# Weight sums by accumulating transfers, ready x parts, one-instruction SiLU and gate rows ahead, in a one-core hybrid decoder layer

## The chip, the core and the metric

The kernel runs on one core of a Trainium2 chip. Its engines run side by side, each through its own list of instructions: TensorE (PE, matrix products), VectorE (DVE), ScalarE (ACT), GpSimd (POOL, here mostly an issuer of transfers) and SyncE (SP, which only issues transfers). An instruction waits for the semaphores of what it depends on, and everything behind it on its engine waits too. The metric is the device time of one execution, in microseconds; the shorter the better.

## The reference: what is computed

One layer for 1024 tokens of width 1024, in float32. The input is normalised and modulated by a conditioning vector to h. One projection of h gives ten pieces: q, f, i and z of an HGRN2 mixer (eight heads), q, k, v, z and a low-rank decay of a gated linear attention (GLA, four heads), and two merge gates.

```python
mod = c_act @ ada_w[l] + ada_b[l]
shift, scale, gate = jnp.split(mod, 3, axis=-1)
h = rms_norm(x, norm_w[l]) * (1.0 + scale[:, None, :]) + shift[:, None, :]
proj = h @ w_in[l]
hq, hf, hi, hz, gq, gk, gv, gz, ga, mg = jnp.split(proj, IN_OFFSETS, axis=-1)
y_h = hgrn2_branch(hq, hf, hi, hz, lb_all[l], hgrn_norm_w[l])
y_g = gla_branch(gq, gk, gv, gz, ga, gla_alpha_w[l], gla_alpha_b[l], gla_norm_w[l])
u_h = y_h @ w_branch[l, 0]
u_g = y_g @ w_branch[l, 1]
mg = jax.nn.sigmoid(mg.reshape(B, T, N_BRANCH, D_MODEL))
merged = mg[:, :, 0] * u_h + mg[:, :, 1] * u_g
x = x + gate[:, None, :] * (merged @ w_out[l])
```

Both mixers are causal linear attentions with a decay per channel (`S = diag(a) S + k v^T`, `o = S^T q`), normalised and multiplied by `silu(z)`; HGRN's q is `silu(hq)`, its k is `(1 - lb) sigmoid(-hf)`. The last step is an RMS norm of x.

## The kernel before

**Products.** Every float32 factor is split in two parts, hi (an ACT cast) and lo (a DVE subtraction, `split` and `pinned_split`, L211 and L212), and a product is hi·hi + hi·lo + lo·hi, so three matmuls. The large products (v and i, the merge gates, the two branches, w_out) are also cut in 2 x 2 blocks and computed with seven block products instead of eight, in the order `PRODUCTS` = 1, 2, 5, 3, 6, 7, 4. Products 1, 2 and 3 use a plain block of h; 5, 7, 6 and 4 use a difference of blocks of h ("x sum", in DRAM as `fx`), and 5, 7, 6 and 3 use a sum of weight blocks.

**Stages on PE, in order.** The head (modulation, transposes of x, h); the q and k features of GLA (L396); V stage 0 (L1899: v of GLA, from 111 us); GLA's z features and the first attentions (L607, scores L665 and L698, outputs L832, L834); V stage 1 (L1899: i of HGRN, about 308 to 405); then the q, f and z features of eight HGRN heads with their attentions (to 778); then the last stages, groups (b, p) of 48 matmuls (L1351) over four column blocks b, the first at 779 us; w_out (L1528); the end norm.

**What sets the order.** `Stream.go` runs a list of jobs (features and V jobs) on PE. `Stream.ahead` issues the loads (SP) and the splits (ACT, DVE) of coming jobs, some jobs ahead and only if enough of the SBUF slots (`S`, 46 of 4 KB per partition) are free. `Stream.weave` advances two tracks by small steps after each unit of PE work: the side track (attention of the current head) and the back track (weight sums, gate row). Each step of a track is a piece of DVE, ACT or transfer work that is thereby put between the others in program order; `held` (`keep_in_program_order`) pins it there. A scheduler orders the rest by priority. Each `yield n` of the back track says after how many units the next step comes.

**The parts that the change touches.**
- `new_factors` (L1161) names the DRAM tiles `fx`. `Vjob.prep` makes the x sums in V stage 0 by a DVE subtraction (`make_factor`, L1739) and stores each by POOL (L1740). V stage 1 and column block 0 of the last stages load them again as float32 (L1843, `fetch_factor`) and split them (L211/L212, L1270/L1271).
- `v_sums` and `prepare` with `weight_sums` load weight blocks by SP, add them on DVE (L1754 to L1760, L1195 to L1201) and store the sums by POOL (L1762, L1203).
- `silu_done` (L967, L968) takes a sigmoid on ACT and multiplies on DVE. The k of HGRN is scaled on DVE (L1104).
- `gate_side` (L1066 to L1083) computes the gate row: eight rows of 512 KB are loaded one at a time, each taken into a DVE multiply-add (L1072), then four matmuls (L1083).
- In V stage 0 PE's results in PSUM are taken out by `Vstage.after` (L1782 to L1810); for product 7 by a DVE addition (L1810), and only then may product 4 start in the same bank.

SP's and POOL's transfers use eight semaphores each in turn, so a transfer waits for the landing of the one eight before it on its queue.

Of the kernel before, what the change touches and what calls it, by code (L numbers as in the profile page):

```python
# [89 lines left out]
def hybrid_trunk_kernel(  # L90
# [117 lines left out]
    def pinned_split(src, hi=None, lo=None):  # L208
        if hi is None:
            hi, lo = (S.get(list(src.shape[1:]), F32R) for _ in range(2))  # L210
        held(nc.scalar.copy(hi, src))  # L211
        nc.vector.tensor_sub(lo, src, hi.bitcast(F32))  # L212
        return hi, lo
# [399 lines left out]
    class Feat:  # L613

        raws, parts, more = 1, 2, 0
# [225 lines left out]
    class Stream:  # L841
# [26 lines left out]
        def go(self, loads=2, preps=1):  # L868
            n = len(self.jobs)
            for i, job in enumerate(self.jobs):  # L870
                self.ahead(i, loads + 2 * job.more, 0)
                for u, _ in enumerate(job.run()):
                    if job.calls(u):
                        self.ahead(i, loads + 2 * job.more, preps + (job.more if u else 0))
# [87 lines left out]
    def silu_done(store, key):  # L962
        def f(ps):
            s = S.get([T])
            for th in range(2):
                sl = slice(th * 512, th * 512 + 512)
                nc.scalar.activation(s[:, sl], ps[th], AF.Sigmoid)  # L967
                nc.vector.tensor_mul(s[:, sl], s[:, sl], ps[th])  # L968
# [93 lines left out]
    def gate_side():  # L1062
# [3 lines left out]
        for k in range(KT):  # L1066
            b = S.get([D])
            nc.sync.dma_start(b, ada_w[0, k * P:(k + 1) * P, 2 * D:3 * D])
            if k == 0:
                nc.vector.tensor_scalar_mul(gacc, b, cs[:, 0:1])  # L1070
            else:
                nc.vector.scalar_tensor_tensor(gacc, b, cs[:, k:k + 1], gacc, ALU.mult, ALU.add)  # L1072
            S.free(b)
            yield 1
# [20 lines left out]
    def hf_done(h):  # L1095
        def fn(ps):
# [7 lines left out]
            nc.vector.tensor_scalar_mul(k, k, oml[:, h:h + 1])  # L1104
# [56 lines left out]
    def new_factors(acts, name):  # L1161
        f = {}
        for p, kh, half in ((1, 0, 0), (2, 1, 0), (3, 1, 1)):
            f[p] = [part_of(acts, kh, half, kk) for kk in range(2)]
        for p in (1, 2, 3, 5, 6, 7, 4):
            if p not in f:
                f[p] = [dp.tile([P, T], F32, name=f"{name}{p}{kk}") for kk in range(2)]
        return f

    f_x = new_factors(h_d, "fx")  # L1170
# [7 lines left out]
    w_sums = [[[dp.tile([P, T], F32, name=f"ws{b}{j}{i}") for i in range(4)] for j in range(2)] for b in range(4)]  # L1178
# [3 lines left out]

    def load_blocks(b, i):
        src = sources[b][i]
        x = [S.get([4, 2, P]) for _ in range(2)]
        for kh in range(2):
            nc.sync.dma_start(x[kh].rearrange("p k a f -> p k (a f)"),
                              src[kh * 512:(kh + 1) * 512, :].rearrange("(k p) f -> p k f", p=P))
        return x

    def weight_sums(b, i, x1, x2):
        s1, s2 = S.get([2, 4, P]), S.get([2, 4, P])
        parts = {5: s1[:, 0], 6: s1[:, 1], 3: s2[:, 0], 7: s2[:, 1]}
        add = nc.vector.tensor_add
        held(add(parts[7], x1[:, :, 0], x1[:, :, 1]))  # L1195
        yield 1
        held(add(parts[5], x1[:, :, 1], x2[:, :, 1]))
        yield 1
        held(add(parts[6], parts[7], x2[:, :, 1]))
        yield 1  # L1200
        held(add(parts[3], parts[6], x2[:, :, 0]))  # L1201
        for p, q in SUMS.items():
            nc.gpsimd.dma_start(w_sums[b][i // 2][q][:, i % 2 * 512:i % 2 * 512 + 512],  # L1203
                                parts[p].rearrange("p k f -> p (k f)"))
        S.free(x1, x2)
        S.free(s1, s2, sent=True)
        summed_up.add((b, i))

    def prepare():
        todo = [(b, i) for b in range(4) for i in range(4)]  # L1210
        blocks_of = {}
        for n in range(len(todo) + 1):
            while n < len(todo) and (len(S.free_list) < 11 or paused[0]):
                yield 1
            if n < len(todo):
                blocks_of[n] = load_blocks(*todo[n])
            if n:
                yield from weight_sums(*todo[n - 1], *blocks_of.pop(n - 1))
            yield 7
# [3 lines left out]
    raw_f, raw_w, wt = {}, {}, {}  # L1223
    GROUPS = [(b, p) for b in range(4) for p in PRODUCTS]
    BUILT = [g for g in GROUPS if g[0] != 1]
# [6 lines left out]

    def fetch_factor(g):
        b, p = g
        raw_f[g] = [S.get([T]) for _ in range(2)]
        for kk in range(2):
            nc.sync.dma_start(raw_f[g][kk], f_x[p][kk])
# [39 lines left out]
    def load_duo(b, p, j):  # L1277

        t = raw_w[b, p, j] = S.get([2, 512])
        if p in SUMS:  # L1280
            assert {(b, 2 * j), (b, 2 * j + 1)} <= summed_up
            nc.sync.dma_start(t.rearrange("p a f -> p (a f)"), w_sums[b][j][SUMS[p]])
# [175 lines left out]
    for g in BUILT[1:]:  # L1458
        n = GROUPS.index(g)
        after(*GROUPS[n - 1], 0, lambda g=g: build(g))  # L1460
        if n > 1 and g[0] == 0:
            after(*GROUPS[n - 2], 2, lambda g=g: fetch_factor(g))
# [254 lines left out]
    vs_d = {p: [dp.tile([P, T], F32, name=f"vs{p}{kk}") for kk in range(2)] for p in SUMS}  # L1717
    summed_v = set()
    W_AT = {1: (0, 0), 2: (1, 0), 5: (0, 1), 3: (1, 0), 6: (0, 1), 7: (0, 0), 4: (1, 1)}
    RAW_X = {1: (0, 0), 2: (1, 0), 3: (1, 1)}  # L1720
# [16 lines left out]
    def make_factor(p, kk):  # L1737
        dst, x, y = {5: ("11", "12", "11"), 7: ("12", "12", "22"), 6: ("22", "22", "11"), 4: ("21", "21", "22")}[p]
        held(nc.vector.tensor_sub(xq[dst][kk], xq[x][kk], xq[y][kk]))  # L1739
        nc.gpsimd.dma_start(f_x[p][kk], xq[dst][kk].rearrange("p a t -> p (a t)"))  # L1740

    def v_sums():

        add = nc.vector.tensor_add
        for kk in range(2):
            while len(S.free_list) < 9:
# [248 lines left out]
```

## Time and profile before

| what | value |
|---|---|
| median of 3 runs | 1176.65 us (1176.1 to 1178.35) |
| the profiled execution, its own time | 1178.0 us |
| its span in the trace | 1176.2 us |
| matmul clock granted | 0.996 |
| POOL transfers of weight sums (L1203) | 64, 545 ns each to issue |
| DMA, 16 engines, mean rate | 188 GB/s, 221.44 MB |

The profile shows one execution. Busy time says how much an engine did, not whether anyone waited for it. PE is the engine that is always needed, so the useful views are those that say when PE stood still and who released it. An engine's timeline row has the start, the duration, the operation and, in brackets, how long the engine was idle before and which engine's work ended that.

### The profile page before, as it was taken

Reading aid. Unit: us, or ns where it says so; the run is one execution under the profiler, and the core shown is the slowest. Engines: PE = TensorE matmul, PEld = TensorE weight load, DVE = VectorE, ACT = ScalarE, POOL = GpSimd, SP = SyncE. Lnnn points to the kernel's source line nnn. Section 1 sums busy time; section 2 is a strip of 40 time slices with the busy share of each in tenths; the row PEclk is TensorE's granted clock in tenths of the full one; section 3 lists DMA queues with packets and bytes.
Section 4 is the critical chain, followed back from the end, with each engine's and each line's share of the span. In section 5 each row is a group of like instructions: output and inputs, shape, how many; then the busy total and the mean of one; then the engine's idle time right before and its main releaser. Section 6 shows DMA issues by size and latency. Waiting matters only on the chain.

```text
span 1176.2 us, 20432 instructions
## 1 busy us (share of the span) xinstructions
PE 1156.2 (98%) x8137; PEld 953.1 (81%) x8137; DVE 849.6 (72%) x1347; ACT 589.5 (50%) x903; POOL 125.0 (11%) x261
## 2 busy tenths in 40 slices
PE   7999999999999999999999999999999999999997
PEld 5777888888888788888888878888888888888886
DVE  4754778567665946897897798795643866988994
ACT  4675464663465535433433425567543644534654
POOL 4121111000100212111111010001110000000000
PEclk8999999999999999999999999999999999999999
DMA  9846445255675856565555453247699846434523
GB/s 319 279 149 233 161 170 189 77 165 171 207 260 177 279 189 201 171 203 173 174 184 188 134 205 112 91 162 241 196 314 298 274 156 215 130 108 162 187 90 134
DMA packets 150802, 221.44 MB, mean 188 GB/s; under 512 B 9052, under 2 KB 107410, under 8 KB 150707
## 3 DMA queue, kind: packets, MB, share of 16 engines
q1 hardware_dynamic: 132114, 158.37, 43.2%
q0 software_dynamic: 18544, 61.76, 13.6%
q8 instruction: 64, 1.05, 0.4%
q14 instruction: 32, 0.25, 0.1%
q10 hardware_dynamic: 48, 0.01, 0.0%
HBM read 154.57 MB, written 65.54 MB: 187 GB/s over the span
## 4 chain that ended last, share of the span: by engine, by line
PE 64%; issue 25%; DVE 4%; POOL 3%; DMA 2%; ACT 1%; SPq 0%; POOLq 0%; DVEq 0%; ACTq 0%
PE pd L607 16%; PE pd L1899 11%; PE pd L1351 9%; PE sc_ps L1351 5%; PE pm L1351 4%; PE pd L1528 3%; PE pd L396 3%; PE sc_ps L1528 2%; PE pm L832 1%; PE pm L1528 1%; POOL ws L1203 1%; PE sc_ps L396 1%; PE pm L834 1%; PE pm L813 1%; DMA b<-qk 1%
## 5 line engine op out<-in xcount | busy, mean ns | idle before, releaser
L607 PE MATMUL pd<-b,b 128*128 128x512 f32 x1632 | 391.1, 395 | 0.2 <-DVE b L212 0.2
L607 PEld LDWEIGHTS pd<-b,b 128*128 128x128 f32 x1632 | 302.1, 188 | 64.3 <-DVE b L212 0.6
L1351 PE MATMUL pd<-b,b 128*128 128x512 f32 x720 | 169.8, 390 | 0.1
L1899 PE MATMUL pd<-b,b 128*128 128x512 f32 x672 | 157.5, 393 | 2.6 <-ACT b L211 1.2
L1351 PEld LDWEIGHTS pd<-b,b 128*128 128x128 f32 x720 | 134.8, 188 | 28.5 <-ACT pd L1334 0.5
L1899 PEld LDWEIGHTS pd<-b,b 128*128 128x128 f32 x672 | 125.3, 188 | 30.5 <-ACT b L211 1.6
L212 DVE TENSOR_TENSOR b<-b,b 128x1024 fp32r<-128x1024 f32 x78 | 94.3, 1221 | 35.0 <-ACT b L211 34.7
L1294 DVE TENSOR_TENSOR b<-b,b 128x1024 fp32r<-128x1024 f32 x56 | 68.4, 1225 | 68.5 <-ACT b L1293 54.4
L1293 ACT CAST b<-b 128x1024 fp32r<-128x1024 f32 x56 | 58.5, 1049 | 69.5 <-PE pm L1351 17.0
L211 ACT CAST b<-b 128x1024 fp32r<-128x1024 f32 x78 | 79.8, 1047 | 12.1 <-DMA v<-b 3.9
L1351 PE MATMUL sc_ps<-b,b 128*128 128x512 f32 x324 | 77.2, 390 | 0.0
L1270 ACT CAST b<-b 128x1024 fp32r<-128x1024 f32 x48 | 49.7, 1049 | 46.5 <-PE pd L1351 16.0
L1351 PE MATMUL pm<-b,b 128*128 128x512 f32 x300 | 71.1, 389 | 0.0
L1351 PEld LDWEIGHTS sc_ps<-b,b 128*128 128x128 f32 x324 | 60.7, 188 | 12.6
L1271 DVE TENSOR_TENSOR b<-b,b 128x1024 fp32r<-128x1024 f32 x48 | 58.0, 1226 | 17.0 <-ACT b L1270 11.5
L1351 PEld LDWEIGHTS pm<-b,b 128*128 128x128 f32 x300 | 56.3, 188 | 11.7
L718 ACT COPY xb<-b 128x512 f32<-128x512 f32 x48 | 29.7, 621 | 55.8 <-DVE b L700 18.9
L1203 POOL DMA_DIRECT2D ws<-b x64 | 34.8, 545 | 190.6 <-DVE b L1195 118.7
L203 DVE TENSOR_TENSOR b<-b,b 128x1024 fp32r<-128x1024 f32 (+1 forms) x37 | 35.9, 984 | 26.4 <-ACT b L202 26.3
L396 PE MATMUL pd<-b,b 128*128 128x512 f32 x192 | 51.9, 403 | 0.5 <-ACT b L202 0.4
L832 PE MATMUL pm<-scT,b 128*128 128x128 f32 x256 | 46.9, 275 | 0.5 <-DVE b L819 0.5
L396 PEld LDWEIGHTS pd<-b,b 128*128 128x128 f32 x192 | 34.3, 188 | 11.6 <-ACT b L202 1.5
(316 smaller groups left out, 1713.3 us busy)
## 6 DMA issues: line engine op xcount, KB each, us to landing
b<-in_w_in_dram SPq DMA_DIRECT2D x72, 512.0 KB, 4.1
ws<-b POOLq DMA_DIRECT2D x64, 256.0 KB, 3.6
b<-ws SPq DMA_DIRECT2D x32, 512.0 KB, 4.6
b<-in_x_dram SPq DMA_DIRECT2D x16, 512.0 KB, 4.2
b<-in_ada_w_dram SPq DMA_DIRECT2D x32, 256.0 KB, 6.5
v<-b POOLq DMA_DIRECT2D x32, 256.0 KB, 4.3
b<-v SPq DMA_DIRECT2D x16, 512.0 KB, 5.0
b<-fx SPq DMA_DIRECT2D x16, 512.0 KB, 4.6
```

What stands on the lines that cost most here:

```text
L211: held(nc.scalar.copy(hi, src))
L212: nc.vector.tensor_sub(lo, src, hi.bitcast(F32))
L396: nc.tensor.matmul(accs[f], wg(a, d, f), b[d][:, half * 512:half * 512 + 512], start=(d == 0 and n == 0), stop=(d == KT - 1 and n == 2))
L607: nc.tensor.matmul(ps[th][0:w, :], a[:, k, 0:w], b[:, th * 512:(th + 1) * 512], start=(k == 0 and n == 0), stop=(k == KT - 1 and n == 2))
L832: nc.tensor.matmul(o, vch(ch)[:, vh * P:(vh + 1) * P], scT[:, ch, :], start=True, stop=(ch == 0))
L1270: nc.scalar.copy(hi, src)
L1271: nc.vector.tensor_sub(lo, src, hi.bitcast(F32))
L1293: nc.scalar.copy(hi, t)
L1294: nc.vector.tensor_sub(lo, t, hi.bitcast(F32))
L1351: nc.tensor.matmul(o, a[:, sl], c, start=(p in (1, 5) and kt == 0 and n == 0), stop=(kt == 3 and n == 2), skip_group_check=True)
L1528: nc.tensor.matmul(o, a, b, start=(p in (1, 5) and kt == 0 and n == 0), stop=(kt == 3 and n == 2), skip_group_check=True)
L1899: nc.tensor.matmul(st.bank[i], x_, w_, start=(p in (1, 5) and kk == 0 and a == 0 and n == 0), stop=(kk == 1 and a == 1 and n == 2), skip_g ...
```

## The change

1. **Weight sums by transfers.** `v_sums` and `prepare` no longer use SBUF and DVE. POOL issues transfers from DRAM to DRAM along a chain of eight steps: the first copies a block, the later ones add onto it (`accum_op=ALU.add`). An adding transfer waits for the landing of the one before it on the same target. The sign of product 3's sum is taken when it is split (`minus_split`).
2. **Both parts of the x sums in DRAM.** V stage 0 stores the hi and lo parts that it has anyway (`xp`, 16 stores of 512 KB, before 8), and V stage 1 and column block 0 load them ready (`load_parts`), with no cast and no subtraction. In column block 0 these loads are issued one group later.
3. **SiLU** is one ACT instruction per half, and k is scaled on ACT.
4. **Gate rows** are loaded two ahead, held in program order, three units apart.
5. **Back track:** `v_sums` goes first, the rest of the decay work follows after 20 units; the first splits of V stage 0 are made a step later (`later`).

```diff
+    def minus_split(src):
+        hi, lo = (S.get(list(src.shape[1:]), F32R) for _ in range(2))
+        held(nc.scalar.activation(hi, src, AF.Copy, scale=-1.0))
+        nc.vector.scalar_tensor_tensor(lo, src, -1.0, hi.bitcast(F32), ALU.mult, ALU.subtract)
...
-                nc.scalar.activation(s[:, sl], ps[th], AF.Sigmoid)
-                nc.vector.tensor_mul(s[:, sl], s[:, sl], ps[th])
+                nc.scalar.activation(s[:, sl], ps[th], AF.Silu)
...
-            nc.vector.tensor_scalar_mul(k, k, oml[:, h:h + 1])
+            nc.scalar.activation(k, k, AF.Copy, scale=oml[:, h:h + 1])
...
-        for k in range(KT):
-            b = S.get([D])
-            nc.sync.dma_start(b, ada_w[0, k * P:(k + 1) * P, 2 * D:3 * D])
...
-            yield 1
+        for k in range(KT + 2):
+            if k < KT:
+                b = S.get([D])
+                nc.sync.dma_start(b, ada_w[0, k * P:(k + 1) * P, 2 * D:3 * D])
+                rows.append(b)
+            if k >= 2:
+                b = rows.popleft()
...
+            yield 3
...
+    CHAIN = ((7, (0, 0)), (5, (0, 1)), (7, (0, 1)), (5, (1, 1)), (6, 7), (6, (1, 1)), (3, 6), (3, (1, 0)))
...
+            for p, src in CHAIN:
+                while paused[0]:
+                    yield 1
+                first = p not in done
+                done.add(p)
+                if isinstance(src, int):
+                    held(nc.gpsimd.dma_start(w_sums[b][p], w_sums[b][src]))
+                else:
+                    for i, x in enumerate(block(*src)):
+                        x = x.rearrange("(k p) f -> p k f", p=P)
+                        y = w_sums[b][p][:, i].rearrange("p (k f) -> p k f", f=P)
+                        if first:
+                            held(nc.gpsimd.dma_start(y, x))
+                        else:
+                            held(nc.gpsimd.dma_start(y, x, accum_op=ALU.add))
+                        yield 1
+                yield 3
...
+    def load_parts(p, kk):
+        x = [S.get([2, 512], F32R) for _ in range(2)]
+        for z in range(2):
+            nc.sync.dma_start(x[z].bitcast(F32).rearrange("p a t -> p (a t)"), xp_d[p][kk][z])
+        return x
...
+    for n, g in enumerate(GROUPS[2:7], 2):
+        after(*((*GROUPS[n - 2], 2) if g[1] in RAW_X else (*GROUPS[n - 1], 0)), lambda g=g: fetch_factor(g))
...
-        nc.gpsimd.dma_start(f_x[p][kk], xq[dst][kk].rearrange("p a t -> p (a t)"))
...
+            self.later = 0 if stage.s else 2
...
+                self.w = minus_split(self.w_raw) if p == 3 else pinned_split(self.w_raw)
...
-                    self.x = pinned_split(self.x_raw)
+                    self.x = load_parts(p, kk)
...
+                for z in range(2):
+                    nc.gpsimd.dma_start(xp_d[p][kk][z], self.x[z].bitcast(F32).rearrange("p a t -> p (a t)"))
...
-        stream.back.append([alpha_side((2, 3)), 72, 1, 0])
         stream.back.append([v_sums(), 2, 1, 0])
+        stream.back.append([alpha_side((2, 3)), 20, 1, 0])
```

**Where instructions moved: the end of V stage 0.** DVE's list before, from the last split of product 7's factors to the first attention's decay products. `pd_0` to `pd_1` are PSUM banks, `xb` holds the attention's q and k, L1810 is the eviction of product 7, and b_1544 is the loaded q/k block.

```order
L212 TENSOR_TENSOR b_1531<-b_849,b_1530 128x1024
L212 TENSOR_TENSOR b_1567<-b_1156,b_1566 128x1024
L212 TENSOR_TENSOR b_1571<-b_1342,b_1570 128x1024
L212 TENSOR_TENSOR b_1607<-b_1157,b_1606 128x1024
L212 TENSOR_TENSOR b_1611<-b_1343,b_1610 128x1024
L1810 TENSOR_TENSOR b_1352<-pd_0_1160,b_1352 128x512
L1810 TENSOR_TENSOR b_1352<-pd_1_1161,b_1352 128x512
L658 TENSOR_TENSOR xb<-b_1544,b_879 128x32x8
L659 TENSOR_TENSOR xb<-b_1544,b_879 128x32x8x2
L1810 TENSOR_TENSOR b_1375<-pd_0_1162,b_1375 128x512
```

And after, where the eviction is L1803 and the q/k block b_1553:

```order
L212 TENSOR_TENSOR b_1538<-b_841,b_1537 128x1024
L664 TENSOR_TENSOR xb<-b_1553,b_871 128x32x8
L665 TENSOR_TENSOR xb<-b_1553,b_871 128x32x8x2
L673 TENSOR_TENSOR b_1553<-b_1553,b_871 128x256
L666 TENSOR_TENSOR xb<-xb,b_871 128x32x16
L212 TENSOR_TENSOR b_1577<-b_1148,b_1576 128x1024
L212 TENSOR_TENSOR b_1581<-b_1341,b_1580 128x1024
L1803 TENSOR_TENSOR b_1351<-pd_0_1152,b_1351 128x512
L212 TENSOR_TENSOR b_1620<-b_1149,b_1619 128x1024
L1803 TENSOR_TENSOR b_1351<-pd_1_1153,b_1351 128x512
```

Four operations on the q/k block and the two splits of product 4's first factors now stand ahead of the first eviction, and one more split between the first two.

POOL's list after, in the same stretch (before, it held only x sums `fx` and v stores here): `xp` are the x parts, `vs` the weight sums, `v` the results.

```order
L1868 DMA xp_781<-b_1413 128x1024
L1868 DMA xp_782<-b_1414 128x1024
L1753 DMA vs_836<-vs_840 16x8192
L1755 DMA vs_835<-in_w_in_dram 256x1x512
L1868 DMA xp_783<-b_1471 128x1024
L1868 DMA xp_784<-b_1472 128x1024
L1755 DMA vs_836<-in_w_in_dram 256x1x512
L1868 DMA xp_785<-b_1509 128x1024
L1782 DMA v_831<-b_1431 128x512 x2
L1782 DMA v_831<-b_1449 128x512 x2
```

The v stores now stand behind adding transfers (L1755) and the parts of products 6 and 7.

**The middle of V stage 1.** DVE before, around the second half of product 7; L1017 is the norm of an attention's output, b_3292 the loaded x sum.

```order
L660 TENSOR_TENSOR xb<-xb,b_2130 128x32x16
L1017 TENSOR_TENSOR b_2568<-b_2568,b_3382 128x256
L1017 TENSOR_TENSOR b_2685<-b_2685,b_3382 128x256
L212 TENSOR_TENSOR b_3481<-b_3290,b_3480 128x1024
L212 TENSOR_TENSOR b_3485<-b_3292,b_3484 128x1024
L1017 TENSOR_TENSOR b_2568<-b_2568,b_3382 128x256
L1017 TENSOR_TENSOR b_2685<-b_2685,b_3382 128x256
L212 TENSOR_TENSOR b_3503<-b_3350,b_3502 128x1024
L1810 TENSOR_TENSOR b_3190<-pd_0_2790,b_3190 128x512
```

After, with L667 the decay product that was L661, and L1022 the norm:

```order
L666 TENSOR_TENSOR xb<-xb,b_2142 128x32x16
L667 TENSOR_TENSOR xb<-xb,b_2142 128x32x8
L673 TENSOR_TENSOR b_3406<-b_3406,b_2142 128x256
L674 TENSOR_TENSOR b_3406<-xb,b_2142 128x256x3
L1022 TENSOR_TENSOR b_2573<-b_2573,b_3362 128x256
L1022 TENSOR_TENSOR b_2678<-b_2678,b_3362 128x256
L212 TENSOR_TENSOR b_3459<-b_3332,b_3458 128x1024
L1022 TENSOR_TENSOR b_2573<-b_2573,b_3362 128x256
L1022 TENSOR_TENSOR b_2678<-b_2678,b_3362 128x256
```

Both splits of product 7's second half are gone from here (its x needs none, its weights' split stands earlier), and the attention's decay products have moved ahead.

**An HGRN attention with gate rows.** DVE before (L1072 is a gate row, L1124 and L1133 the former head's output, L661 the product that PE's score block L665 reads):

```order
L1201 TENSOR_TENSOR b_6429<-b_6428,b_6241 128x512
L212 TENSOR_TENSOR b_6510<-b_6285,b_6509 128x1024
L1133 TENSOR_TENSOR b_4662<-b_4662,b_6472 128x1024
L658 TENSOR_TENSOR xb<-b_6280,b_6445 128x32x8
L659 TENSOR_TENSOR xb<-b_6280,b_6445 128x32x8x2
L667 TENSOR_TENSOR b_6280<-b_6280,b_6445 128x256
L660 TENSOR_TENSOR xb<-xb,b_6445 128x32x16
L1072 SCALAR_TENSOR_TENSOR b_6684<-b_6705,cs,b_6684 128x1024
L661 TENSOR_TENSOR xb<-xb,b_6445 128x32x8
```

And after, for the same head:

```order
L664 TENSOR_TENSOR xb<-b_6095,b_6257 128x32x8
L665 TENSOR_TENSOR xb<-b_6095,b_6257 128x32x8x2
L1134 SCALAR_TENSOR_TENSOR b_5977<-pm_6287,vec,b_5977 128x512
L212 TENSOR_TENSOR b_6318<-b_6098,b_6317 128x1024
L1143 TENSOR_TENSOR b_4569<-b_4569,b_6284 128x1024
L666 TENSOR_TENSOR xb<-xb,b_6257 128x32x16
L673 TENSOR_TENSOR b_6095<-b_6095,b_6257 128x256
L667 TENSOR_TENSOR xb<-xb,b_6257 128x32x8
```

The weight addition L1201 is gone and the gate row has moved to the next head.

More of the change, by code (lines that the diff above doesn't have):

```diff
@@ L613, in hybrid_trunk_kernel @@
     class Feat:
-        raws, parts, more = 1, 2, 0
+        raws, parts, more, later = 1, 2, 0, 0
         def calls(self, u):
@@ L873, in go @@
                     if job.calls(u):
-                        self.ahead(i, loads + 2 * job.more, preps + (job.more if u else 0))
+                        self.ahead(i, loads + 2 * job.more, preps + (job.more if u >= job.later else 0))
                     if (n - i, u) in self.hooks:
@@ L1159, in part_of @@
         return acts[half][kh * 2 + kk]
[L1161 to L1170, printed above, removed]
+    xp_d = {p: [[dp.tile([P, T], F32, name=f"xp{p}{kk}{z}") for z in range(2)] for kk in range(2)]
+            for p in (5, 6, 7, 4)}
     def branch(n, d):
@@ L1191, in weight_sums @@
[L1191 to L1207, printed above, removed]
@@ L1906, in run @@
             if p not in RAW_X:
-                S.free(*self.x)
+                S.free(*self.x, sent=not st.s)
     first_loads = {(2, 0): [lambda: load_xq(0)],
```

111 lines of the change are left out of this document (47 added, 64 removed).

## The prediction

> **What bounds the kernel now.** First the page: busy time by engine, and the span in 40 slices.
>
> ```profile
> PE 1156.2 (98%) x8137; PEld 953.1 (81%) x8137; DVE 849.6 (72%) x1347; ACT 589.5 (50%) x903; POOL 125.0 (11%) x261
> PE   7999999999999999999999999999999999999997
> ```
>
> TensorE (PE) is busy 98%; only the first and last slices are not full. Relief for VectorE (DVE) can help in two ways: PE runs faster beside it, or PE waits less. Two stretches of the view by windows settle the first (PE, PEld, DVE, ACT, POOL busy us; clock, DMA share, GB/s):
>
> ```profile
> 120.00:150.00 30.00, 30.00 (x134) 24.82 (x134) 21.07 (x18) 15.03 (x20) 3.77 (x7) 1.00 0.38 141
> 930.00:1080.00 150.00, 150.00 (x663) 124.22 (x662) 116.11 (x124) 70.57 (x84) 0.00 (x0) 1.00 0.49 163
> ```
>
> With DVE 70% and 77% busy, and POOL issuing or silent, PE starts a matmul every 224 ns (30/134) and 226 ns (150/663). Its rate does not hang on them, so only waits count. The view of PE's waits (total us, times, longest):
>
> ```profile
> PE pm L423 <- DVE b L225: 4.6, 2, 3.8
> PE pm L160 <- DMA rows_c<-in_c_dram: 2.4, 1, 2.4
> PE pd L1899 <- ACT b L211: 1.2, 1, 1.2
> PE pd L1899 <- DVE b L364: 0.8, 1, 0.8
> ...
> PE sc_ps L665 <- DVE xb L661: 0.7, 1, 0.7
> PE pd L1899 <- DVE b L212: 0.6, 1, 0.6
> PE pm L832 <- DVE b L819: 0.5, 1, 0.5
> ...
> PE sc_ps L698 <- DVE xb L694: 0.4, 1, 0.4
> ...
> PE pm L1083 <- DVE b L819: 0.2, 1, 0.2
> PE pd L607 <- DVE b L212: 0.2, 1, 0.2
> ```
>
> L423, L160 and L1899 after L364 lie ahead of every changed instruction. The change can reach 1.2 + 0.7 + 0.6 + 0.5 + 0.4 + 0.2 + 0.2 = **3.8 us**, 0.3%. That caps the gain, however many DVE instructions go.
>
> **The change part by part.** The sum is made against the profiled execution's 1178.0 us (span 1176.2 and 1.8 around it) and then carried to the median of the runs, 1176.65.
>
> *Ready x parts in V stage 1.* PE's timeline at the longest reachable wait (start, us, operation; idle before it in brackets), then the load that the change doubles, from the list of DMA issues (KB, us to landing):
>
> ```profile
> 386.50 0.82 PE L1899 MATMUL pd<-b,b 128*128 128x512 f32 x2 [1.17 <-ACT b L211]
> 387.95 1.42 PE L1899 MATMUL pd<-b,b 128*128 128x512 f32 x5 [0.64 <-DVE b L212]
> ```
>
> ```profile
> b<-fx SPq DMA_DIRECT2D x16, 512.0 KB, 4.6
> ```
>
> The second half of product 7 waits for its x factor's cast and then for its subtraction. Both go; the parts come from DRAM. They are loaded up to two jobs ahead, 2 x 24 matmuls x 224 ns = 10.8 us, against 2 x 4.6 us even if two loads follow one another: hidden, and nothing is late next, since the weights' split now stands earlier. **-1.8 us** (1.17 + 0.64). For the score block behind it (0.4) DVE has three subtractions fewer, but the block comes eight matmuls (1.8 us) earlier on PE; with L607's 0.2, which a lighter DVE should shorten, I count half of 0.6: **-0.3 us**.
>
> *Gate rows and weight sums.* DVE ahead of the 0.7 us wait, and the group of POOL's stores of weight sums (count | busy us, mean ns | idle before and its releasers):
>
> ```profile
> 686.19 1.27 DVE L1072 SCALAR_TENSOR_TENSOR b<-b,cs,b 128x1024 f32<-128x1024 f32 x1
> 687.39 0.63 DVE L661 TENSOR_TENSOR xb<-xb,b 128x256 f32<-128x256 f32 x1
> ```
>
> ```profile
> L1203 POOL DMA_DIRECT2D ws<-b x64 | 34.8, 545 | 190.6 <-DVE b L1195 118.7
> ```
>
> ```profile
> 190.00:640.00 450.00, 447.32 (x3880) 373.95 (x3868) 325.30 (x596) 214.96 (x344) 55.77 (x103) 1.00 0.58 186
> ```
>
> A gate row of 1.27 us sits right before the decay product that PE waits for. In the order after the change no row and no weight addition is left before it (POOL no longer waits 118.7 us for L1195 either): **-0.7 us**. The gate matmuls of L1083 move behind other work: **-0.2 us**. The wait at L832 hangs on a chain of state updates that keeps its place: 0, at best -0.5.
>
> The sums themselves become transfers within DRAM. No row of this trace shows an accumulating transfer. It can be no worse for the end than the old sums (0 or a gain) as long as it lands in time; the nearest row, a 512 KB load, takes 4.6 us, and if reading the target, adding and writing it each took that, 14 us. I take 4.6, the only row. The merge and branch sums run in the stretch of the last row, 190 to 640, and are wanted only in the last stages, behind the HGRN features, so even 14 us each is off the path. POOL queues v, y and gate stores behind a waiting accumulation; what waits for those is a buffer or a load well ahead of its use. 0, with the crowding of DMA (0.58 there) as rival 4.
>
> *SiLU and k on ACT.* The multiplications, the table loads of the SiLU line, and the HGRN stretch:
>
> ```profile
> L968 DVE TENSOR_TENSOR b<-b,pd 128x512 f32<-128x512 f32 x48 | 31.1, 684 | 15.0 <-ACT b L967 15.0
> ...
> L967 ACT ACT_TABLE_LOAD x6 | 7.7, 1283 | 0.1
> ```
>
> ```profile
> 410.00:778.00 368.00, 366.92 (x3536) 306.14 (x3535) 291.00 (x550) 157.29 (x278) 44.54 (x82) 1.00 0.53 170
> ```
>
> DVE loses 31.1 us. The order shows 47 table loads for 30, so ACT gains 17 x 1.283 = 21.8 us, and eight k scalings of 1.05 us (as the copy of the same size, L657, in the next part). In the HGRN stretch (410 to 778) ACT is 157/368 = 43% busy and would be near 51%, DVE falls from 79%: 0. The idle before those six loads is 0.1 us in all, so a load costs its own 1.28 us here. The Trainium skill, "ScalarE: Activation LUTs", section "What ACT_TABLE_LOAD costs", adds a drain of about 1.38 us to each load. By that figure ACT's extra would be about 45 us, still under the idle of that stretch, so it speaks against the SiLU edit and leaves the sum as it is.
>
> *The new order in V stage 0.* Here I expect a loss. The timelines before: DVE, ACT, SP's queue, PE.
>
> ```profile
> 174.45 1.23 DVE L212 TENSOR_TENSOR b<-b,b 128x1024 fp32r<-128x1024 f32 x1 [1.14 <-ACT b L211]
> 175.59 1.28 DVE L1810 TENSOR_TENSOR b<-pd,b 128x512 f32<-128x512 f32 x2
> 176.79 0.64 DVE L658 TENSOR_TENSOR xb<-b,b 128x256 f32<-128x256 f32 x1
> 177.31 0.87 DVE L659 TENSOR_TENSOR xb<-b,b 128x512 f32<-128x512 f32 x1
> 178.64 0.86 DVE L660 TENSOR_TENSOR xb<-xb,b 128x512 f32<-128x512 f32 x1
> 181.67 0.68 DVE L667 TENSOR_TENSOR b<-b,b 128x256 f32<-128x256 f32 x1
> ```
>
> ```profile
> 156.52 3.89 ACT L211 CAST b<-b 128x1024 fp32r<-128x1024 f32 x4
> ...
> 172.42 1.05 ACT L657 COPY xb<-b 128x1024 f32<-128x1024 f32 x1 [0.37 <-DMA b<-qk]
> ```
>
> ```profile
> 162.26 3.78 SPq L1029 DMA_DIRECT2D b<-qk  x2
> ```
>
> ```profile
> 176.71 2.66 PE L1899 MATMUL pd<-b,b 128*128 128x512 f32 x11
> ```
>
> The first product-4 matmul is the second of those eleven, at 176.71 + 0.24 = 176.95, and needs its bank emptied by the first L1810 (over at 176.2). After the change four operations of the first attention (the old L658, L659, L667, L660) and two splits stand ahead of that eviction on DVE. They need the q/k block whose load is issued at the end of SP's row (166.0) and lands at 172.4. From a landing at 172.4: 0.64 + 0.87 + 0.68 + 0.86 + 2 x 1.23 + 0.64 = 6.15 us, less about 0.1 us of overlap at each of six joints: 5.5, so 177.9 and a stall of 1.0 us. It grows one for one with a later landing. DMA there:
>
> ```profile
> 153.00:162.00 9.00, 9.00 (x42) 7.44 (x41) 4.40 (x4) 8.20 (x12) 0.00 (x0) 1.00 0.01 3
> 162.00:183.00 21.00, 21.00 (x152) 17.24 (x151) 19.27 (x24) 6.93 (x7) 5.39 (x10) 1.00 0.97 324
> ```
>
> From 162 on DMA is full. By POOL's order some 5 MB (x parts, sums, v) can be issued before the q/k load, where 2 MB were. The first x part may leave when its cast ends (156.52 + 1.05 = 157.6), so of the 3 MB more the idle DMA up to 162 takes 4.4 us x 0.324 = 1.4 MB. The rest, 1.6 MB, is 5 us at 324 GB/s if it goes ahead of the load, 2.5 if both queues share the engines; on the other side the second q/k load (0.5 MB, 1.6 us) no longer stands in front. So the landing moves by +0.9 to +3.4 us, or by -1.6 if the extra traffic is gone in time. I take +1, the value nearest to the row of before, where the load landed in an equally full DMA: the stall is 1.0 + 1.0 = **+2.0 us**, with ends 0 and 4.4. "DMA: Bandwidth & Descriptors", section "Queues, rings and completion order", in the Trainium skill has each DMA engine take turns between queues packet by packet; by it the extra traffic costs the load 2.5 us and not 5, the landing moves by 2.5 - 1.6 = +0.9, and the sum would be 0.1 us lower; without it, at 5 - 1.6 = +3.4, 2.4 us higher. No row of this trace tells the two apart.
>
> *x parts in the last stages, first column block.* Eight casts and subtractions leave; groups 5, 6, 7 and 4 load 2 MB instead of 1, one group later.
>
> ```profile
> 842.00:850.00 8.00, 8.00 (x37) 6.64 (x36) 5.81 (x7) 4.88 (x7) 2.67 (x5) 1.00 0.61 190
> 850.00:870.00 20.00, 20.00 (x90) 16.57 (x89) 10.80 (x12) 7.71 (x11) 5.36 (x11) 1.00 0.99 352
> 853.50 1.30 PE L1351 MATMUL pd<-b,b 128*128 128x512 f32 x5
> ```
>
> Group 4 is the tight one: loads issued when its predecessor starts, 48 matmuls (10.8 us) before 853.5, so at 842.7. 2.1 MB at 352 GB/s take 6 us beside the 1.5 MB (190 GB/s x 8 us) already moving there, 4 more: done at 853 with nothing to spare. 0, with an end at +3.
>
> **Sum:** -1.8 - 0.3 - 0.7 - 0.2 + 2.0 = -1.0 us: 1177.0 for the profiled execution, **1175.6** on the median's scale. A measurement of this kernel tells about 0.2% (2.35 us) from no change.
>
> **Rivals.**
> 1. *No new stall.* The q/k block lands by 171.4 and the waits go: -3.0 to -3.8, 1172.9 to 1173.7. For it: SP's queue holds less ahead of that load. Against: DMA at 0.97.
> 2. *Slower: the first attention's load is the new bound.* It lands 4 us late, at 176.4, since x parts and sums fill POOL's queue; the stall is 5, and the same doubling makes group 4 late by up to 3 near 853: -3.0 + 5 + 3 = +5, 1181.6; with the first alone 1178.7. It decides from a landing 4 us late. For it: 0.97 and 0.99.
> 3. *ACT tables.* Silu and sigmoid alternate in each of eight heads; if one load of 1.28 us per head falls ahead of a cast that PE waits for, and half of it is covered, 8 x 0.64 = 5 us: 1180.7. Against: 43% busy.
> 4. *Sums crowd the feature loads* from 190 to 640: rows of 512 B, four blocks of 24 transfers of 512 rows, 49,000 of them, where 32 loads of 512 rows and 64 stores of 128 made 25,000, at a share of 0.58 already. Four features late by 1 us: 1179.6. Against: features are loaded two ahead (2 x 10.8 us).
> 5. *The waits stay*, because a chain other than the removed one ends as late: 1176.6 to 1178.
>
> **How the numbers follow.** Forecast 0.38 (own range 1173.6 to 1177.2; 0.12 of it under 1174.3); rival 1 0.26; rival 2 0.17 (0.14 over 1179.0); rivals 3 and 4 0.07 each (0.06 over); rival 5 0.05. Faster: 0.12 + 0.26 = 0.38; slower: 0.14 + 0.06 + 0.06 = 0.26; the rest, 0.36, is within 0.2%. Range 1172.6 to 1181.5: rival 1 with its best end below, most of rivals 2 to 4 above.
>
> **What would show it.** PE's waits after: no L1899 on an ACT cast or on the split of an x factor near 386, no wait behind a gate row near 687, and a new one of 1 to 3 us on the eviction (now L1803) near 177, with ACT's copy of the q/k block just before at 172 to 175. Rival 1 shows none there; rival 2 shows it at 5 and DMA at 0.95 from 157 on. Waits on ACT in the HGRN stretch would mean rival 3, on feature loads rival 4. A changed 224 ns per matmul would overthrow the whole reading.

## The result, and the profile after

The changed kernel is slower: 1190.43 us median against 1177.5 for the kernel before in the same comparison, a ratio of 1.010 (95% interval 1.0084 to 1.0117). Forecast were 1175.6 us and a range of 1172.6 to 1181.5. One of the four executions of the changed kernel took 1648.3 us at a granted clock of 0.654; the median counts it and the ratio leaves it out, and the median of the other three is 1189.1.

PE's waits after (engine, waiting line, releaser; total us, times, longest):

```profile
PE pd L1891 <- DVE b L1803: 11.6, 1, 11.6
PE pm L429 <- DVE b L231: 4.3, 2, 3.0
PE pm L160 <- DMA rows_c<-in_c_dram: 2.4, 1, 2.4
PE pm L797 <- DVE b L732: 1.8, 1, 1.8
PE pm L819 <- ACT b L798: 1.1, 1, 1.1
PE pd L1891 <- DVE b L370: 0.8, 1, 0.8
PE pd L402 <- ACT b L202: 0.4, 1, 0.4
```

All seven waits within the change's reach are gone, from L665 to L607. In their place stands one of 11.6 us, at the place of the forecast stall: the eviction of product 7 (L1803) before product 4. Two smaller ones, L797 and L819, are new. The chain behind the long one on SP, ACT, DVE and PE (start, us, operation; idle before it in brackets):

```profile
164.60 0.32 SPq L1034 DMA_DIRECT2D b<-qk  x1
```

```profile
181.91 1.04 ACT L663 COPY xb<-b 128x1024 f32<-128x1024 f32 x1 [20.22 <-DMA b<-qk]
182.87 5.07 ACT L211 CAST b<-b 128x1024 fp32r<-128x1024 f32 x5
```

```profile
181.91 0.64 DVE L664 TENSOR_TENSOR xb<-b,b 128x256 f32<-128x256 f32 x1 [13.82 <-DMA b<-qk]
182.45 0.87 DVE L665 TENSOR_TENSOR xb<-b,b 128x512 f32<-128x512 f32 x1
183.19 0.63 DVE L673 TENSOR_TENSOR b<-b,b 128x256 f32<-128x256 f32 x1
183.72 0.87 DVE L666 TENSOR_TENSOR xb<-xb,b 128x512 f32<-128x512 f32 x1
184.49 2.36 DVE L212 TENSOR_TENSOR b<-b,b 128x1024 fp32r<-128x1024 f32 x2
186.75 0.70 DVE L1803 TENSOR_TENSOR b<-pd,b 128x512 f32<-128x512 f32 x1
```

```profile
187.60 6.78 PE L1891 MATMUL pd<-b,b 128*128 128x512 f32 x18 [11.63 <-DVE b L1803]
```

The order of DVE is the one shown with the change, and from the landing to PE's restart it takes 187.60 - 181.89 = 5.7 us (5.5 were worked out). What is far off is the landing: the load is issued at 164.6, as early as before, and lands 17.3 us later; before it took some 6.7.

The 18 matmuls after the wait take 6.78 us, not 18 x 0.224 = 4.0: the granted clock there is half (last section). So this place costs 11.6 + 2.7 us, L797 and L819 2.9; the seven waits that went gave 3.8, and the head happened to wait 0.9 less. That is 12.5 of loss; the spans differ by 1187.0 - 1176.2 = 10.8, so 1.7 us more were gained than the rows of this view show (a wait here costs more than its row, see the first point on the prediction).

### The profile page after: what moved, and what is told of

It reads as the page before. It is cut to its first block, busy times and chain, and to the rows that moved or that the text cites. A ratio compares the mean times of both kernels' runs of the same rounds, so it can differ in the third digit from the quotient of the medians.

```text
span 1187.0 us, 20172 instructions
## 1 busy us (share of the span) xinstructions
PE 1157.4 (98%) x8137; PEld 955.0 (80%) x8137; DVE 754.7 (64%) x1203; ACT 603.5 (51%) x912; POOL 216.2 (18%) x317
## 4 chain that ended last, share of the span: by engine, by line
PE 91%; DMA 4%; DVE 2%; ACT 1%; issue 1%; SPq 0%; POOL 0%; DVEq 0%; ACTq 0%
PE pd L613 31%; PE pd L1352 14%; PE pd L1891 10%; PE sc_ps L1352 6%; PE pm L1352 6%; PE pd L402 3%; PE pd L1529 3%; PE pm L838 2%; DMA b<-qk 2%; PE pm L840 2%; PE pm L819 2%; PE sc_ps L1529 2%; PE sc_ps L402 2%; PE pm L1529 1%; PE sc_ps L671 1%; DMA xp<-b 1%
## 5 line engine op out<-in xcount | busy, mean ns | idle before, releaser
L613 PEld LDWEIGHTS pd<-b,b 128*128 128x128 f32 x1632 | 302.0, 188 | 63.9
L1891 PE MATMUL pd<-b,b 128*128 128x512 f32 x672 | 159.5, 396 | 12.5 <-DVE b L1803 11.6
L1891 PEld LDWEIGHTS pd<-b,b 128*128 128x128 f32 x672 | 127.0, 190 | 40.6 <-ACT b L211 12.0
L1352 PEld LDWEIGHTS pd<-b,b 128*128 128x128 f32 x720 | 134.8, 188 | 28.1 <-ACT pd L1335 0.2
L1295 DVE TENSOR_TENSOR b<-b,b 128x1024 fp32r<-128x1024 f32 x56 | 68.3, 1222 | 71.1 <-ACT b L1294 54.9
L212 DVE TENSOR_TENSOR b<-b,b 128x1024 fp32r<-128x1024 f32 x68 | 82.5, 1222 | 43.8 <-ACT b L211 43.2
L1294 ACT CAST b<-b 128x1024 fp32r<-128x1024 f32 x56 | 58.5, 1052 | 67.0 <-PE pm L1352 17.3
L211 ACT CAST b<-b 128x1024 fp32r<-128x1024 f32 x68 | 69.8, 1045 | 5.9 <-issue 3.2
L1352 PEld LDWEIGHTS pm<-b,b 128*128 128x128 f32 x300 | 56.3, 188 | 11.7
L1271 ACT CAST b<-b 128x1024 fp32r<-128x1024 f32 x40 | 41.5, 1054 | 38.7 <-PE pd L1352 14.8
L1272 DVE TENSOR_TENSOR b<-b,b 128x1024 fp32r<-128x1024 f32 x40 | 48.1, 1219 | 12.6 <-ACT b L1271 8.6
L732 DVE TENSOR_TENSOR b<-b,tot 128x512 f32<-128x512 f32 x36 | 24.7, 687 | 43.3 <-PE sc_ps L773 43.1
L1206 POOL DMA_DIRECT2D ws<-in_w_in_dram x32 | 43.5, 2195 | 34.0 <-DMA ws<-ws 32.0
```

Source lines behind the costliest of these rows:

```text
L613: nc.tensor.matmul(ps[th][0:w, :], a[:, k, 0:w], b[:, th * 512:(th + 1) * 512], start=(k == 0 and n == 0), stop=(k == KT - 1 and n == 2))
L1206: held(nc.gpsimd.dma_start(y, x, accum_op=ALU.add))
L1294: nc.scalar.copy(hi, t)
L1295: nc.vector.tensor_sub(lo, t, hi.bitcast(F32))
L1352: nc.tensor.matmul(o, a[:, sl], c, start=(p in (1, 5) and kt == 0 and n == 0), stop=(kt == 3 and n == 2), skip_group_check=True)
L1891: nc.tensor.matmul(st.bank[i], x_, w_, start=(p in (1, 5) and kk == 0 and a == 0 and n == 0), stop=(kk == 1 and a == 1 and n == 2), skip_g ...
```

## The experiments

Times are medians; ratios are to the kernel before, on the same chip.

| run | what | us | ratio (95% interval) |
|---|---|---|---|
| e1 | change, V sums after V stage 0 | 1172.6 | 0.9953 (0.9938 to 0.9968) |
| e2 | change without ready x parts | 1179.27 | 1.0019 (0.9999 to 1.0040) |
| e3 | change, first q/k load earlier | 1195.76 | 1.0155 (1.0133 to 1.0177) |
| e4 | before + SiLU, k, gate rows | 1177.45 | 0.9999 (0.9989 to 1.0009) |
| e5 | change, V sums copied and not added | 1177.1 | 0.9988 (0.9978 to 0.9998) |
| e6 | change, order at the eviction fixed | 1182.69 | 1.0042 (1.0025 to 1.0058) |
| e7 | e1 without SiLU and k on ACT | 1174.18 | 0.9967 (0.9955 to 0.9979) |
| e8, e12 | e1 with e6's order, the same kernel twice | 1172.2, 1172.59 | 0.9951 (0.9937 to 0.9964), 0.9957 (0.9944 to 0.9969) |
| e9 | e8 and single transfers behind its end | 1248.74 | |
| e10 | change, V sums one unit apart | 1185.5 | 1.0071 (1.0054 to 1.0089) |
| e11 | change, all weight sums on DVE | 1175.53 | 0.9983 (0.9974 to 0.9992) |

**e1: the sums' traffic taken out of V stage 0.**

```diff
-        stream.back.append([v_sums(), 2, 1, 0])
-        stream.back.append([alpha_side((2, 3)), 20, 1, 0])
+        stream.back.append([v_sums(), 56, 1, 0])
+        stream.back.append([alpha_side((2, 3)), 0, 1, 0])
...
-                yield 3
+                yield 1
```

> The changed kernel, with the V weight sums started after V stage 0 instead of at its beginning (56 units later, one unit between transfers); DVE's order at the eviction of product 7 stays as changed. Theory A (the sums' transfers fill DMA, so the first q/k load lands 9.5 us later and the eviction behind it on DVE with it): the load lands by 172 to 176, the stall at the eviction falls from 11.6 us to 1 to 4, the time to 1177 to 1181. Theory C (the doubled x-part stores alone fill DMA): the load still lands at 179 or later, the stall stays above 8, the time above 1186. Either way the sums now run beside the first attention, and the second q/k load may be late there by 1 to 3 us.

The load is issued at the same time and lands in 5.4 us (SP, then ACT):

```profile
164.56 0.32 SPq L1034 DMA_DIRECT2D b<-qk  x1
```

```profile
169.98 1.05 ACT L663 COPY xb<-b 128x1024 f32<-128x1024 f32 x1 [8.32 <-DMA b<-qk]
```

No wait at the eviction is left, though the four attention operations still stand ahead of it on DVE: theory A, and the time is better than the 1177 to 1181 expected. Doubled x-part stores alone (C) do no harm here. At the second attention, where the sums now run, L797 still waits 0.6 us and L819 1.1. From 140 to 165 the view by windows (the last three columns are clock, DMA share, GB/s) has before, after and e1 in this order:

```profile
140.00:165.00 25.00, 25.00 (x112) 20.72 (x111) 16.75 (x16) 17.75 (x23) 2.29 (x5) 1.00 0.23 77
```

```profile
140.00:165.00 25.00, 25.00 (x112) 20.72 (x111) 17.88 (x17) 16.08 (x21) 7.57 (x12) 1.00 1.06 288
```

```profile
140.00:165.00 25.00, 25.00 (x112) 20.72 (x111) 17.91 (x17) 16.07 (x21) 4.28 (x8) 1.00 0.42 158
```

After the change DMA is full over the whole stretch ahead of the load, where its share had been 0.23.

**e2: the x sums as before, the adding transfers kept.** Eight float32 stores, loads and splits as in the kernel before (`f_x` for `xp_d`); DVE's order at the eviction then is that of before.

> The changed kernel with the x sums in DRAM as before (8 stores of float32, loaded and split again), the sums by accumulating transfers kept. This puts DVE's order at the eviction back to that of before. Theory B (the order is what costs): no wait at the eviction even though the q/k load lands late (176 or later); what is left is a wait of the score block behind it of at most the landing after 175, so 1 to 5 us, and the waits near 386 come back (+1.8): 1178 to 1184. Theory A: the same order, but the load is late by the sums alone; if it lands before 175 there is no wait at all: 1176 to 1178. If x parts alone were the load's trouble (C), it lands by 173.

```profile
PE pd L1887 <- DVE b L1797: 1.5, 1, 1.5
PE pd L1887 <- ACT b L211: 1.4, 1, 1.4
PE pd L1343 <- DVE b L1286: 1.2, 1, 1.2
```

A wait of 1.5 us at the eviction (L1797) remains, where theory B had none; the one near 386 is back, as expected; a new one in the last stages (L1286, an x split at 854 that the ready parts had removed) was not foreseen. The load lands at 173.2, 8.8 us after its issue, although DMA's share from 140 to 165 is 0.98. DVE's order differs from the change here, so it is this landing, not the wait, that tells of the stores: without the parts the sums alone delay the load little, and the 17.3 us take both.

**e3: the q/k load earlier.**

```diff
-    vjobs[0][10].begins = lambda: load_qk(0)
+    vjobs[0][6].begins = lambda: load_qk(0)
```

> The changed kernel with the load of the first head's q/k block started four V jobs earlier (job 6 instead of 10); everything else stays. All traffic stays. Theory A and B both: the load lands ahead of its use, the eviction is no longer held, the 11.6 us stall goes and the half clock after it: 1190.4 - 11.6 - 2.8 = 1176, or 1175 if the first attention runs ahead. If the stall had another cause (the splits of product 4 held by stores that land late), 3 us or more remain: 1179 or more.

A clear miss: some 6 us slower than the change, each against the kernel before. PE's waits, and ACT ahead of the longer one:

```profile
PE pd L1891 <- DVE b L1803: 10.7, 1, 10.7
PE pd L1891 <- DVE b L212: 5.2, 1, 5.2
```

```profile
193.64 1.99 ACT L211 CAST b<-b 128x1024 fp32r<-128x1024 f32 x2 [12.53 <-DMA b<-in_w_in_dram]
```

The q/k load now holds up a split at 154, and at the eviction another load (a feature's weights) has taken its place in front on ACT. With DMA full, the early load only passes the delay on to another.

**e4: SiLU, k and gate rows alone, in the kernel before.** The edits are those of the diff at L968, L1104 and in `gate_side`.

> The kernel before, with only the SiLU instruction, k scaled on ACT and the gate rows two ahead. My account: the waits of 0.7 us near 687 and 0.2 near 719 go, nothing new, 1 us faster than before. Rival (table loads delay casts in the HGRN stretch): waits on ACT casts in 410 to 778, 3 to 6 us slower.

No change (0.9999), and no wait on a cast in the HGRN stretch. The gate row's wait went, but its matmuls got one of their own, and the x split at 854 came late by 0.7:

```profile
PE pd L1355 <- DVE b L1298: 0.7, 1, 0.7
...
PE pm L1087 <- ACT b L1089: 1.5, 1, 1.5
```

**e5: copies for additions.** This leaves out the additions in the V sums: products 5, 6, 7 and 3 of V stage 1 use single blocks.

```diff
-                    held(nc.gpsimd.dma_start(y, x, accum_op=ALU.add))
+                    held(nc.gpsimd.dma_start(y, x))
```

> The changed kernel with the eight adding transfers of the V weight sums made plain copies (no addition; the weights of products 5, 6, 7 and 3 in V stage 1 are then single blocks). Same number of bytes written, same order, same waits. If adding as such is slow (reading the target), DMA between 140 and 165 is no longer full (share 1.0 to 1.1 before this), the q/k load lands by 176 and the stall is 5 or less: 1183 or less. If bytes and rows are what fill it, the load lands at 179 or later and the stall stays at 8 or more: 1187 to 1191.

```profile
PE pd L1891 <- DVE b L1803: 2.5, 1, 2.5
```

```profile
140.00:165.00 25.00, 25.00 (x112) 20.72 (x111) 17.43 (x17) 16.55 (x22) 6.37 (x12) 1.00 0.90 315
```

```profile
173.23 1.05 ACT L663 COPY xb<-b 128x1024 f32<-128x1024 f32 x1 [11.08 <-DMA b<-qk]
```

The decisive run. The transfers, the bytes that they write, their order and the waits are the same, and the load lands at 173.2 instead of 181.9; the stall is 2.5 us and the time some 13 us lower, each against the kernel before. It is the adding as such: with it DMA is busy 1.06 for 288 GB/s, without it 0.90 for 315.

**e6: the order fixed, the traffic kept.** The first attention's copy on ACT and three products on DVE, and L1803, pinned in program order:

```diff
+        pin = held if me == 1 else (lambda x: x)
+        pin(nc.scalar.copy(xb[:, :, 0:32], q.rearrange("p (b t) -> p b t", t=32)))
+        pin(TT(X[:, :, :, 0], q4[:, :, :, 1], f4[:, :, :, 1], M))
+        pin(TT(X[:, :, :, 1:4:2], q4[:, :, :, 2:4], f4[:, :, :, 2:4], M))
...
+        pin(TT(q4[:, :, :, 0], q4[:, :, :, 0], f4[:, :, :, 0], M))
...
+                held(nc.vector.tensor_add(t, bank, t))
```

> The changed kernel with the first attention's operations on its q/k block (one copy on ACT, three products on DVE) pinned behind the casts of product 4 and the evictions of product 7. All traffic stays. Theory: late load times order. The load still lands near 182, but nothing waits for it except the score block; this needs the landing + 1.3 + 0.9 + 0.6 = 185 where it stood at 180 to 181, so PE waits 3 to 4 us there instead of 11.6, and keeps more of its clock: 1190.4 - 14.4 + 4 = 1180. If the full DMA holds back something else that product 4 needs, the wait stays above 8: 1187 or more.

```profile
PE pd L1892 <- DVE b L1804: 6.8, 2, 4.0
...
PE sc_ps L672 <- DMA b<-qk: 3.2, 1, 3.2
```

```profile
175.12 1.99 ACT L211 CAST b<-b 128x1024 fp32r<-128x1024 f32 x2 [5.53 <-DMA v<-b]
182.65 1.04 ACT L664 COPY xb<-b 128x1024 f32<-128x1024 f32 x1 [5.54 <-DMA b<-qk]
```

The score block waits 3.2 us, as expected, but the eviction still 6.8: a cast for product 4 needs a buffer that a v store has to leave, and that store is late too; then the copy of the q/k block holds the next cast on ACT. Pinning the order won back some 7 us of the loss; the rest stays as long as the transfers are late.

**e7: e1 without SiLU and k on ACT** (those two edits undone).

> The kernel of e1 (late V sums) with SiLU as sigmoid and DVE product again and k scaled on DVE. In e1 a table load of 1.28 us and two SiLU halves stand on ACT ahead of the copy that PE waits for at 208 (1.1 us). If the table load makes that wait, it goes or halves: 0.5 to 1 us faster than e1, 1171.6 to 1172.1. If SiLU on ACT pays through a lighter DVE, waits come back in the HGRN stretch: 1173 to 1174.

The wait of 1.1 us at L819 is there as in e1, so the table load does not make it, and the expected gain does not come. The kernel is 1.6 us slower by the medians, on another chip; the intervals overlap, so SiLU on ACT is no loss and perhaps a gain.

**e8 and e12: e1 with the order of e6.**

> The kernel of e1 with the order of e6 as well. In e1 nothing waits at the eviction, so the pinning has nothing to gain there: the same as e1 within 0.1%, 1172 to 1173.5. If the operations on the q/k block ahead of the eviction did help the score block, it is late by about 1 us: 1173.5.

> e8 once more, beside e11 on the same chip: 1172 to 1173, 0.4 to 0.6% under the kernel before; no wait at the eviction, none longer than 1.2 us after the head.

As expected, the same as e1, and no wait at the eviction. The score block (L672) now waits 1.1 us in e8 and 1.3 in e12, a little more than e12's 1.2. With e1 this is the best kernel here, 0.4 to 0.5% faster than the one before and some 1.4% faster than the change.

**e9: the transfers' own cost**, one at a time behind the end of the kernel (`za`, `zb` are scratch tiles in DRAM):

```diff
+    for _ in range(4):
+        held(nc.gpsimd.dma_start(za, w2, accum_op=ALU.add))
+    for _ in range(4):
+        held(nc.gpsimd.dma_start(za, w2))
...
+    for _ in range(4):
+        held(nc.gpsimd.dma_start(y1, w1, accum_op=ALU.add))
+    for _ in range(4):
+        held(nc.gpsimd.dma_start(y1, w1))
```

> The kernel of e8 with a chain of transfers behind its end, one at a time on an otherwise idle DMA: four adding transfers of 512 KB (rows of 2 KB, as the V sums), four plain copies of the same blocks, four adding and four plain ones of 256 KB in rows of 512 B (as the merge sums). The time itself grows by the chain, some 80 to 130 us. Theory: adding is slower as such: 6 to 9 us to landing for an adding 512 KB against 4 to 5 plain, 1.3 to 2 times the DMA time. Rival: alone they cost the same within 10%, and the difference of e5 comes only from adding in a full DMA.

Landing times by source line (min, median, max) of 512 KB adding, then plain:

```profile
DMA to landing us min/median/max: 5.9/6.7/9.3
```

```profile
DMA to landing us min/median/max: 4.0/4.0/4.2
```

And what the software queue moved in 22 us (three adding transfers) and in the last 7 of them (one), in 17 us (four plain), then in 24 and 14 us (four each of 256 KB in rows of 512 B, adding and plain); columns are packets, MB, share of the 16 engines:

```profile
q0 software_dynamic: 816, 1.57, 49.7%
```

```profile
q0 software_dynamic: 272, 0.52, 48.8%
```

```profile
q0 software_dynamic: 576, 2.10, 40.9%
```

```profile
q0 software_dynamic: 2112, 1.05, 46.1%
```

```profile
q0 software_dynamic: 320, 1.05, 26.2%
```

Over three, an adding transfer of 512 KB takes 0.497 x 22 / 3 = 3.6 us of all engines, but two of them run beside the kernel's own output stores (the landing of 9.3 is one of these). The last one, nearly alone (1173 to 1180), lands in 5.9 us and takes 0.488 x 7 = 3.4; a plain copy takes 0.409 x 17 / 4 = 1.7. So adding takes 2.0 times the engine time of copying. In rows of 512 B it is 0.461 x 24 / 4 = 2.8 against 0.262 x 14 / 4 = 0.9, 3.0 times, with 528 packets for 80. The landing (5.9 for 4.0) shows less of it than the share does.

**e10: the sums close together at the beginning.**

```diff
-                yield 3
+                yield 1
...
-        stream.back.append([alpha_side((2, 3)), 20, 1, 0])
+        stream.back.append([alpha_side((2, 3)), 52, 1, 0])
```

> The changed kernel with the same 16 V sum transfers at the same start but one unit apart instead of three, so that they are over sooner; DVE's order at the eviction and all the other work stay. Theory (a queue of adding transfers still unfinished when the q/k load goes out): they are done by about 160, the load lands by 172 to 175, the stall is 1 to 3 us: 1176 to 1179. Rival (the order on DVE, or the amount of traffic in V stage 0 as a whole): the stall stays above 8, 1187 or more; loads of V stage 0 itself may then be late too.

```profile
PE pd L1891 <- ACT b L211: 4.3, 1, 4.3
...
PE pd L1891 <- DVE b L1803: 1.0, 1, 1.0
```

At the eviction the theory holds: the load, now issued at 172.6, lands in 6.6 us and the stall is 1.0. But the time, 1185.5, is above the expectation: the crowd now delays V stage 0 itself (4.3 us near 142), which is also why the load is issued 8 us later than in the change. This trace is of the fastest execution, 1180.46; the median is 5 us higher.

**e11: all weight sums on DVE again**, the rest as changed; `v_sums`, `prepare` and the back order as before.

> The changed kernel with all weight sums on DVE again, as before (part 1 of the change and its place in the back track undone); ready x parts, SiLU, k and gate rows as changed. DVE's order at the eviction is the changed one. Theory: without adding transfers the q/k load lands by 171 to 173, the stall at the eviction is 0 to 1.5 us although four attention operations stand ahead of it, and the other gains stay: 1172.5 to 1175. Rival (the order on DVE costs by itself): a stall of 3 us or more, 1177 or more. If it is as fast as e12, the transfers bring nothing; if it is 1 to 2 us slower, their gain is the additions taken off DVE.

Again no wait at the eviction, with the four operations ahead of it. So the order alone costs nothing. Two other waits came (1.6 and 1.2 us). Next to it on the same chip e12 is 2.9 us faster: transfers for the sums do pay, by about that, where they stand in nobody's way (e12 also pins the order, which gained nothing in e8 over e1).

## Why the prediction was wrong

- **Only waits count, 3.8 us at most to gain: the seven waits went, but the cap was too low.** The change with the V sums late and the order pinned (e8) is 5.8 us faster than the kernel before, 4.2 to 7.4 by its interval. Here a wait costs more than the idle time in its row. Before, 57 matmuls of V stage 1 lie between 379.72 and the score block at 395.26, with two waits of 1.17 and 0.64 among them: 15.5 us. After, 48 lie between 395.59 and the score block at 406.56: 11.0 us, or 0.229 each. At that rate 57 take 13.0, so the waits cost 2.5 us where their rows show 1.8. The first rows of the two stretches:

```profile
379.72 5.61 PE L1899 MATMUL pd<-b,b 128*128 128x512 f32 x24
```

```profile
395.59 11.05 PE L1891 MATMUL pd<-b,b 128*128 128x512 f32 x48
```

- **The place of the loss: right.** Eviction behind four attention operations and two splits, held by the first q/k load, 5.5 us from landing to restart (5.7 measured).
- **Its size: wrong, and this is the step that failed.** The stall was put at 2.0 us, with an upper end of 4.4; it was 11.6, and 2.7 more in clock. The working bounded an adding transfer by 4.6 and 14 us to landing, took 4.6, "the only row", and used the range only where the merge and branch sums are wanted. For V stage 0 it counted bytes at 324 GB/s, 1.6 us for 512 KB, and let the idle DMA up to 162 take 1.4 MB. Alone, an adding transfer takes 3.4 us of all engines (e9), and in the changed kernel the V sums' eight landed after 7.7 to 15.5 us. Six are issued ahead of the load: 6 x (3.4 - 1.7) = 10 us more than as many copies. So nothing was idle (1.06 from 140 to 165), and the load found a queue. With plain copies (e5) the forecast's numbers come out nearly: stall 2.5 and 1.2 us under the kernel before, where 2.0 and 1.0 were forecast. That is partly luck: from 140 to 165 e5 moved 315 GB/s x 25 us = 7.9 MB where the kernel before moved 1.9, so 6 MB more and not the 3 that the working counts.
- **How the two queues share the engines was wrong too.** The working halves the 5 us of extra traffic if both queues share. From 166 to 178 the view of DMA (packets, MB, share of 16 engines) has POOL's queue, q0, and SP's, q1, of the changed kernel and then of e5:

```profile
q0 software_dynamic: 1017, 3.63, 88.5%
q1 hardware_dynamic: 980, 0.51, 15.8%
```

```profile
q0 software_dynamic: 848, 3.35, 68.2%
q1 hardware_dynamic: 1946, 1.44, 36.2%
```

  In the changed kernel the two queues move nearly the same number of packets, but POOL's are 3.6 KB on average and SP's 0.5, so SP's queue gets 12% of the bytes. The small packets are the rows of a feature load (L595) issued at 162.27, ahead of the q/k load; it lands after 18.4 us, and the q/k load 1.3 us behind it. In e5 POOL's queue takes 68% of the engines' time and not 88%, and SP's moves twice the packets. This is read from the traces; no run exchanges the two loads and keeps the rest. In e3, where the q/k load goes out before the feature loads, it takes some 9 us with DMA at 1.07.
- **A second place was missed.** DVE and PE at the second attention, of the changed kernel:

```profile
217.53 0.64 DVE L664 TENSOR_TENSOR xb<-b,b 128x256 f32<-128x256 f32 x1 [9.40 <-DMA b<-qk]
218.06 0.87 DVE L665 TENSOR_TENSOR xb<-b,b 128x512 f32<-128x512 f32 x1
218.80 0.68 DVE L732 TENSOR_TENSOR b<-b,tot 128x512 f32<-128x512 f32 x1
```

  The next head's q/k block is late as well, and L732, which PE's L797 needs, stands behind it: 1.8 us.
- **Rival 2 was the right mechanism** with too low a price: the landing came 9.5 us late where 4 was its case.
- **The rule on turns between queues** ("DMA: Bandwidth & Descriptors", section "Queues, rings and completion order", in the Trainium skill) was weighed as +0.9 us for the landing, and +3.4 without it. The trace agrees with turns by packet (1017 and 980), but the measured landing, +9.5, fits neither value: both rested on the same count of bytes, and equal turns are not equal bytes.
- **Rival 3 did not happen** (e7: L819's wait stays without SiLU; no cast is waited for in the HGRN stretch). **Rival 4 neither**: DMA's share from 190 to 640 rose from 0.58 to 0.77 and the merge sums' transfers took 9.0 us at the median, but no feature load is among PE's waits.
- **Group 4 of the last stages** was in time: no wait there.

What stays open is why SP's queue moved only 2 packets from 162 to 166, before the turns began, and why SP took 11.7 us to issue the q/k load's second half at 166.98, where 0.36 is usual; and e10's spread (1180.5 to 1187.2).

## What to carry to other kernels

An operation that no row shows needs its whole range carried into every place where it runs, above all as load on a shared resource: not only "when does it land" but "how much of the DMA does it take from others". Ahead of a load that an in-order engine waits for, ask what the queues hold, not only when the load is issued, and whether a transfer of many small rows stands in front of it on its own queue; moving that load earlier (e3) or the sums closer (e10) moved the delay, and moving the extra traffic to a stretch that waits for nothing (e1) removed it. A moved instruction that is harmless while its data is early (e1, e11) turns into the bound when it is late.

## What the runs showed of the hardware

- Adding in a DRAM to DRAM transfer costs 2.0 times (2 KB rows) to 3.0 times (512 B rows) the engine time of a copy (e9).
- With both queues full, the changed kernel moved 1017 packets of POOL's queue and 980 of SP's from 166 to 178; with packets of 3.6 and 0.5 KB that is 3.63 MB against 0.51.
- After a long wait PE restarts at half the clock. After 11.6 us in the changed kernel (first row) and after 4.3 in e10 (second) it is 0.50 over the 4.4 and 5.0 us of these rows; after 2.7 us in e6 (third) it is 1.00.

```profile
187.60:192.00 4.40, 4.40 (x10) 3.44 (x11) 4.40 (x7) 0.33 (x1) 2.87 (x6) 0.50 0.64 183
```

```profile
143.00:148.00 5.00, 4.64 (x11) 3.67 (x12) 3.64 (x4) 1.53 (x2) 1.07 (x1) 0.50 1.02 276
```

```profile
178.20:182.50 4.30, 4.30 (x18) 3.24 (x18) 2.16 (x3) 0.00 (x0) 2.17 (x4) 1.00 1.03 399
```
